# Issue order in a gated DeltaNet scan and of the first two input transfers, in a hybrid encoder layer

## The chip, the cores and the metric

The kernel runs on one core of one Trainium2 chip. The metric is device time in microseconds, the median of several runs. The engines named below are TensorE (PE in the profile, with its weight loads as PEld), VectorE (DVE), ScalarE (ACT), GpSimd (POOL) and SyncE (SP), whose queue issues most of the DMA transfers.

## The reference

One encoder layer over 16 meta tokens and 1024 tokens of width 1024, in float32. A normed input is multiplied with one wide matrix; its columns feed a bidirectional gated DeltaNet with 8 heads (branch A), a short convolution (branch B) and two merge gates. Then come the branch projections, an output projection and a SwiGLU block. The change sits in branch A's scan, which the reference writes as follows, once forwards and once over the reversed sequence:

```python
def step(S, inp):
    qk_c, qd_c, kd_c, u_c, w_c, gl_c = inp
    v_new = u_c - jnp.einsum("bhcd,bhde->bhce", w_c, S)
    o_c = (jnp.einsum("bhcd,bhde->bhce", qd_c, S)
           + jnp.einsum("bhij,bhje->bhie", qk_c, v_new))
    S = S * gl_c[..., None, None] + jnp.einsum("bhcd,bhce->bhde", kd_c, v_new)
    return S, o_c
```

Here u_c and w_c come from a solve with a unit lower triangular matrix, whose inverse the kernel builds beforehand.

## The kernel before

The layer has three stretches. In the first, up to about 923 us, the input projection runs as a stream of dense products (line 328: 128 x 128 weights against 320 to 512 columns, each float32 product split in three), while eight heads pass through norms, inverses and scans beside it. Two further stretches hold the branch projections and the SwiGLU block.

In the first stretch each engine's order of work is the order in which the program issues it, and a small planner decides that order while the program is being built. It keeps a clock for each engine in a table `T`. `pe(ns)` moves TensorE's clock and returns it plus 200; `V(n, kind)` and `A(n)` add an operation's planned time to VectorE's or ScalarE's clock, no earlier than TensorE's, and return that clock plus 370. A stream (the decay, the norms, the inverse or the scan of a head) is a generator. When it yields a time, the main loop goes on with dense products until TensorE's clock has reached it, and only then resumes the stream. `pump()` hands VectorE waiting jobs (convolutions, forward substitutions, norms) while its clock is less than 700 ahead. The planner runs while the kernel is built; on the chip only the order is left, and the semaphores.

A head's scan (`g_scan`, from line 774) takes 8 chunks of 128 tokens in 8 steps; step i works on chunk i forwards and chunk 7 - i backwards. Eight heads make 64 steps. In the first step the backward direction has no state yet, so only the forward one takes part in the products with the state. A step runs so:

- line 853: keys times state, into a PSUM bank b1; line 856: queries times state, into a bank b2
- line 863, VectorE: r0 = values minus the decayed b1, one operation for each direction
- `late`: the product of the step before that is still owed (`inner`, line 892, scores times new values); `outputs()`: its sums into the output on VectorE (line 839) and, once a chunk has been seen from both sides (the outputs of steps 4 to 7, which are issued one step later), their squares on ScalarE (line 843)
- line 871: the inverse (`NP`) times r0, into the other half of b2
- lines 878 and 883, ScalarE: w and v2, two scalings of that result
- line 888: keys times w, into b1; line 902, VectorE: the new state S
- lines 831 and 834: the query part of the output, on ScalarE or VectorE

The scan's PSUM banks come from a ring of three. Each float32 product of the scan shows as two TensorE records, so a group over both directions has four.

At the start of the program nine tiles of 128 rows of x, of 512 KB each, are requested on SP's queue. Tile 0 holds the 16 meta rows and the first 112 rows of x, so two transfers fill it (lines 1049 and 1050). Each tile is squared and summed on ScalarE (line 1073), scaled on VectorE (lines 161 to 168 and 1082) and transposed on TensorE (line 98); the first dense product of line 328 needs three tiles. Before it scales the first tile, VectorE copies the norm's weights out of PSUM (line 1150).

Of the kernel before, what the change touches and what calls it, by code (L numbers as in the profile page):

```python
# [16 lines left out]
P = 128  # L17
# [3 lines left out]
META = 16  # L21
# [27 lines left out]
def encoder_layer(ctx: ExitStack, tc: tile.TileContext, x, meta, norm1_w, w_in, w_ba,  # L49
                  dn_conv_w, A_log, dt_bias, dn_norm_w, sc_conv_w, w_bdn, w_bsc,  # L50
                  w_out, norm2_w, w_gu, w_down, final_w, out):
    nc = tc.nc
    x, out = x[0], out[0]
# [11 lines left out]
    def uid(s):  # L65
        cnt["n"] += 1
        return f"{s}_{cnt['n']}"
# [27 lines left out]
    mm = nc.tensor.matmul  # L95
# [155 lines left out]
    T = {"pe": 0.0, "dve": 0.0, "act": 0.0, "pool": 0.0}  # L251

    def on(e, ns, ready=0.0):

        T[e] = max(T[e], ready, T["pe"]) + ns
        return T[e] + TOPE

    def pe(ns):
        T["pe"] += ns
        return T["pe"] + HOP  # L260

    def V(n, kind=0):
        return on("dve", (68 + 1.042 * n, 130 + 1.042 * n, 130 + 0.52 * n)[kind])

    def A(n):
        return on("act", 144 + 0.834 * n)
# [204 lines left out]
    def cs(c):  # L471
        return slice(META + c * P, META + (c + 1) * P)
# [301 lines left out]
    def g_scan(h, st_):  # L774
        nonlocal freed
        kq, vT, small, kn, NP, PQ, Pm = (st_[k] for k in ("kq", "vT", "small", "kn", "NP", "PQ", "Pm"))
        kT, qT = kq[:, 0], kq[:, 1]
# [6 lines left out]
        def newbank():  # L784
            return pss().rearrange("p (a n) -> p a n", a=4)
# [25 lines left out]
        S = [S0, None]  # L811
# [3 lines left out]
        def outputs():  # L815

            while pending:
                pending.pop(0)()

        def output(b2, c, d, sums):  # L820
            eg = eG[:, c, (h, 8 + h)[d]:(h, 8 + h)[d] + 1]
            first = c not in seen
            seen.add(c)
            if not sums:
                def copy():
                    nc.scalar.copy(oacc[c], b2[:, 2 + d])
                    A(P)
                pending.append(copy)
                return
            if first:  # L830
                nc.scalar.activation(oacc[c], b2[:, d], AF.Copy, scale=eg)
                A(P)
            else:
                nc.vector.scalar_tensor_tensor(out=oacc[c], in0=b2[:, d], scalar=eg, in1=oacc[c],
                                               op0=ALU.mult, op1=ALU.add)
                V(P, 1)

            def add_up():
                nc.vector.tensor_tensor(out=oacc[c], in0=b2[:, 2 + d], in1=oacc[c], op=ALU.add)  # L839
                V(P)  # L840
                if not first:
                    jk = dn.tile([P, P], F32, tag="jk", name=uid("jk"))
                    nc.scalar.activation(jk, oacc[c], AF.Square, accum_out=sso[:, c:c + 1])  # L843
                    on("act", 310)
            pending.append(add_up)

        for i in range(NC):
            cd = (i, NC - 1 - i)
            hd = (h, 8 + h)
            act_ = [d for d in range(2) if S[d] is not None]  # L850
            b1, b2 = newbank(), newbank()
            for d in act_:
                mm(b1[:, d], kT[:, cs(cd[d])], S[d], start=True, stop=True)
            t = pe(215 * len(act_))
            for d in act_:
                mm(b2[:, d], qT[:, cs(cd[d])], S[d], start=True, stop=True)
            pe(215 * len(act_))
            yield t
            r0 = [vS[:, cd[0]], vS[:, cd[1]]]
            for d in act_:  # L860
                c = cd[d]
                r0[d] = dn.tile([P, P], F32, tag=f"r{d}", name=uid("r0"))
                nc.vector.scalar_tensor_tensor(out=r0[d], in0=b1[:, d], scalar=negEG[:, c, hd[d]:hd[d] + 1], in1=vS[:, c],
                                               op0=ALU.mult, op1=ALU.add)
                t = V(P, 1)
            while late:
                late.pop(0)()
            outputs()
            yield t
            for d in range(2):  # L870
                mm(b2[:, 2 + d], NP[:, cd[d], d], r0[d], start=True, stop=True)  # L871
            yield pe(430)
            w = [None, None]
            v2 = [None, None]
            for d in range(2):
                c = cd[d]
                w[d] = dn.tile([P, P], F32, tag=f"w{d}", name=uid("w"))
                nc.scalar.activation(w[d], b2[:, 2 + d], AF.Copy, scale=ce[:, c, d:d + 1])  # L878
                t = A(P)
            for d in range(2):  # L880
                c = cd[d]
                v2[d] = dn.tile([P, P], F32, tag=f"v2{d}", name=uid("v2"))
                nc.scalar.activation(v2[d], b2[:, 2 + d], AF.Copy, scale=cc[:, c, d:d + 1])
                tv = A(P)
            if i < NC - 1:
                yield t
                for d in range(2):
                    mm(b1[:, d], kn[:, cd[d]], w[d], start=True, stop=True)
                t = pe(430)
            def inner(b2=b2, cd=cd, v2=v2):  # L890
                for d in range(2):
                    mm(b2[:, 2 + d], PQ[:, cd[d], d], v2[d], start=True, stop=True)
                return pe(430)
            if i < NC - 1:
                late.append(inner)
                yield t
                for d in range(2):
                    Sn = dn.tile([P, P], F32, tag=f"S{d}", name=uid("S"), bufs=2)
                    if S[d] is None:
                        nc.vector.tensor_copy(Sn, b1[:, d])  # L900
                    else:
                        nc.vector.scalar_tensor_tensor(out=Sn, in0=S[d], scalar=eGl[:, cd[d], hd[d]:hd[d] + 1],
                                                       in1=b1[:, d], op0=ALU.mult, op1=ALU.add)
                    t = V(P, 1)
                    S[d] = Sn
            else:
                yield tv
                t2 = inner()
                freed += 1
                yield t2  # L910

            for d in range(2):
                output(b2, cd[d], d, d in act_)
            yield t
# [50 lines left out]
    def pick():  # L965

        mid = fill_units and fill_units[0][3] in (1, 2)
        if qkv_units and not mid and qkv_ok():
            u = qkv_units.pop(0)
        elif fill_units:  # L970
            u = fill_units.pop(0)
        else:
            return None
        raw = rawtile([P, KT, P])
        nc.sync.dma_start(raw, w_in[unit(u[0])])
        return [u, None, raw, [0]]
# [11 lines left out]
    def start_streams():  # L988
        nonlocal ndec, nnorm, ninv, nscan
        h = ndec  # L990
        if h < H and h < freed + 2 and not decs:
            decs.append([g_decay(h, heads[h]), T["dve"] + HOP, h])
            ndec += 1
        h = nnorm
        if h < H and h < ndec and h < freed + 2 and not norms and all(k in heads[h] and heads[h][k]() for k in ("tk", "tq")):
            norms.append([g_norm(h, heads[h]), T["dve"] + HOP, h])
            nnorm += 1
        h = ninv
        if h < H and not invs and heads[h].get("normed"):
            invs.append([g_inv(h, heads[h]), T["dve"] + HOP, h])  # L1000
            ninv += 1
        h = nscan
        if h < H and not scans and heads[h].get("inverted") and "tv" in heads[h] and heads[h]["tv"]():
            scans.append([g_scan(h, heads[h]), T["dve"] + HOP, h])
            nscan += 1
# [22 lines left out]
    with tc.tile_pool(name="st", bufs=1) as st:  # L1028
# [17 lines left out]
        units = []  # L1046
        for t, xr in enumerate(xs):
            if t == 0:
                nc.sync.dma_start(xr[:META], meta)
                nc.sync.dma_start(xr[META:P], x[0:P - META])  # L1050
            else:
                nc.sync.dma_start(xr[:size(t)], x[P * t - META:P * t - META + size(t)])
            if t == 2:
                units.append(pick())

                nc.sync.dma_start(rows[:120, 0], dn_conv_w[0].rearrange("k (t p) -> (k t) p", p=P))
                nc.sync.dma_start(rows[:24, 1], sc_conv_w[0].rearrange("k (t p) -> (k t) p", p=P))
                nc.sync.dma_start(rows[24:25, 1], dn_norm_w)
                nc.sync.dma_start(raw, w_ba)
            elif t == 5:  # L1060
                units.append(pick())
# [585 lines left out]
    for n, j in enumerate(range(GH + 2, KT - 1), 2):  # L1647
        d = pair_steps(n, j)[0]
# [82 lines left out]
    for t in range(KT - 1):  # L1731
# [3 lines left out]
        xr = m3[2]  # L1735
# [67 lines left out]
    t = KT - 1  # L1803
# [14 lines left out]
    xr = m3[2]  # L1818
# [330 lines left out]
```

## Time and profile before

| | |
|---|---|
| time, median of 3 runs | 1973.54 us (1972.09 to 1974.93) |
| the profiled execution's own time | 1973.36 us |
| its span, first to last instruction | 1971.6 us |
| granted TensorE clock | 1.000 |
| idle time of TensorE before a product, longest single case | 1.5 us, at the start |

The busy shares in the page are averages over the whole span. A busy TensorE row says that products were in flight; how dense they are is read from the distance of their starts in the time-ordered view. There a row joins neighbouring records of one line, with the start of the first, the time to the end of the last, and their number; an idle time ahead of a row stands in brackets with what ended it.

### The profile page before, as it was taken

The numbers are of one execution on the slowest core, as the hardware profiler recorded it, in microseconds if no ns is written. First come the engines' busy times: TensorE is split into PE (matmuls) and PEld (weight loads), VectorE is DVE, ScalarE is ACT, GpSimd is POOL, SyncE is SP. The second block draws the span as 40 slices with busy tenths as digits, with TensorE's granted clock in tenths as the row PEclk, the third lists the DMA queues.
The fourth block names the chain that finished last, engine by engine and source line by source line (L and its number), as shares of the span: only waits on it lengthen the run. The fifth ranks groups of instructions, "written<-read, shape, count | busy, mean of one in ns | idle before, by whom it ended". The sixth has DMA issues, their size and how long they took to land.

```text
span 1971.6 us, 31923 instructions
## 1 busy us (share of the span) xinstructions
PE 1957.3 (99%) x11992; PEld 1719.6 (87%) x11992; DVE 1398.0 (71%) x3017; ACT 837.7 (42%) x1968; POOL 108.4 (5%) x410
## 2 busy tenths in 40 slices
PE   9999999999999999999999999999999999999998
PEld 8999999999999999888888888888888888878887
DVE  7888688888888888845954544468676765746575
ACT  6462364646464646343444211235333333324344
POOL 2011101010101010100000000000000000000000
PEclk9999999999999999999999999999999999999999
DMA  4122121212121212223246642133366654577654
GB/s 145 61 86 81 55 87 60 77 59 77 59 84 52 87 49 87 65 81 108 85 150 242 245 153 86 65 107 112 103 234 246 245 189 153 178 274 242 193 173 168
DMA packets 124704, 251.53 MB, mean 128 GB/s; under 512 B 44988, under 2 KB 46453, under 8 KB 122117
## 3 DMA queue, kind: packets, MB, share of 16 engines
q1 hardware_dynamic: 123957, 248.44, 37.8%
q8 instruction: 94, 1.54, 0.3%
q10 hardware_dynamic: 592, 1.05, 0.1%
q14 instruction: 61, 0.50, 0.1%
HBM read 181.20 MB, written 68.25 MB: 127 GB/s over the span
## 4 chain that ended last, share of the span: by engine, by line
PE 45%; DMA 3%; DVE 2%; ACT 1%; issue 0%; SPq 0%; DVEq 0%; ACTq 0%
PE pd L1446 12%; PE pe L1446 6%; PE pm L1446 4%; PE pe L2057 1%; PE pe L2055 1%; PE pe L2056 1%; PE pd L2057 1%; PE pd L2055 1%; PE pd L2056 1%; PE pe L134 1%; PE pe L135 1%; PE pd L135 1%; PE pd L134 1%; PE pe L136 1%; PE pd L136 1%; PE pm L2056 1%
## 5 line engine op out<-in xcount | busy, mean ns | idle before, releaser
L328 PE MATMUL pm<-hTh,wh 128*128 128x320 f32 (+4 forms) x1248 | 426.9, 347 | 0.3 <-ACT hTh L1096 0.2
L328 PE MATMUL pm<-hTh,wl 128*128 128x320 f32 (+4 forms) x1248 | 426.8, 347 | 0.0
L328 PE MATMUL pm<-al,wh 128*128 128x320 f32 (+4 forms) x1248 | 423.8, 345 | 0.0
L328 PEld LDWEIGHTS pm<-hTh,wh 128*128 128x128 f32 x1248 | 233.9, 188 | 10.7 <-ACT hTh L1096 0.9
L328 PEld LDWEIGHTS pm<-al,wh 128*128 128x128 f32 x1248 | 233.8, 188 | 10.7
L328 PEld LDWEIGHTS pm<-hTh,wl 128*128 128x128 f32 x1248 | 233.9, 188 | 10.2 <-POOL wl L1111 0.3
L102 DVE TENSOR_TENSOR al<-raw,ring_h 128x1024 fp32r<-128x1024 f32 x73 | 88.6, 1222 | 65.6 <-ACT ring_h L101 64.7
L101 ACT CAST ring_h<-raw 128x1024 fp32r<-128x1024 f32 x73 | 76.6, 1053 | 109.1 <-PE pe L2057 35.0
L982 DVE TENSOR_TENSOR wl<-raw,wh 128x512 fp32r<-128x512 f32 x112 | 75.3, 687 | 34.5 <-ACT wh L985 34.2
L350 DVE SCALAR_TENSOR_TENSOR kq<-ra,wc,kq 128x520 f32<-128x520 f32 x128 | 96.5, 754 | 3.5 <-ACT kq L380 2.0
L878 ACT ACTIVATE w<-pd,small 128x128 f32<-128x128 f32 x128 | 39.8, 362 | 123.4 <-PE pd L871 122.9
L483 DVE TENSOR_TENSOR tm<-fP,fN 128x135 f32<-128x135 f32 (+23 forms) x248 | 72.2, 291 | 4.8
L487 DVE TENSOR_TENSOR fP<-fP,tm 128x135 f32<-128x135 f32 (+23 forms) x248 | 71.9, 290 | 5.0
L985 ACT CAST wh<-raw 128x512 fp32r<-128x512 f32 x112 | 66.3, 624 | 3.8 <-issue 3.6
L101 ACT CAST wh<-raw 128x1024 fp32r<-128x1024 f32 x37 | 38.8, 1047 | 47.8 <-PE pe L135 10.4
L1994 ACT ACTIVATE b<-b 128x512 f32<-128x512 f32 x20 | 12.6, 632 | 101.6 <-DVE b L1412 101.6
L843 ACT ACTIVATE jk<-NP 128x128 f32<-128x128 f32 x64 | 19.9, 311 | 81.1 <-DVE NP L839 80.1
L102 DVE TENSOR_TENSOR wl<-raw,wh 128x1024 fp32r<-128x1024 f32 x37 | 45.1, 1219 | 10.2 <-ACT wh L101 10.0
L1446 PE MATMUL pd<-b_hl,wh 128*128 128x512 f32 x168 | 51.9, 390 | 0.0
L1412 DVE TENSOR_TENSOR b<-pd,b 128x512 f32<-128x512 f32 x21 | 14.5, 689 | 52.5 <-PE pd L1446 47.5
L350 DVE SCALAR_TENSOR_TENSOR vT<-ra,wc,vT 128x520 f32<-128x520 f32 x64 | 48.3, 754 | 1.4 <-ACT vT L380 0.7
L679 POOL TENSOR_TENSOR tm<-mP,mN 1x15 f32<-1x15 f32 (+7 forms) x120 | 36.9, 307 | 210.8 <-DMA mN<-ndm 202.4
(630 smaller groups left out, 4772.1 us busy)
## 6 DMA issues: line engine op xcount, KB each, us to landing
raw<-in_w_in_dram SPq DMA_DIRECT2D x72, 512.0 KB
raw<-in_w_gate_up_dram SPq DMA_DIRECT2D x44, 512.0 KB
sums<-in_w_down_dram SPq DMA_DIRECT2D x22, 512.0 KB
t_d<-sums SPq DMA_DIRECT2D x11, 1024.0 KB
raw<-s_d SPq DMA_DIRECT2D x44, 256.0 KB
raw<-t_d SPq DMA_DIRECT2D x44, 256.0 KB
act_d<-b SPq DMA_DIRECT2D x43, 256.0 KB
raw<-act_d SPq DMA_DIRECT2D x33, 256.0 KB
```

Source lines behind the costliest of these rows:

```text
L101: nc.scalar.copy(hi, src)
L102: nc.vector.tensor_tensor(out=lo, in0=src, in1=hi.bitcast(F32), op=ALU.subtract)
L134: mm(po[:m, :n], wh[:, k, :m], xhk[:, t0:t0 + n], start=(k == 0), stop=False)
L328: mm(po[:, :n], ww[:, k], f(k)[:, t0:t0 + n], start=i == 0, stop=i == 3 * KT - 1)
L350: nc.vector.scalar_tensor_tensor(out=acc, in0=raw[:, h0 + t:h0 + t + hn], scalar=wc[:, t, col:col + 1], in1=acc, op0=ALU.mult, op1=ALU.add)
L483: nc.vector.tensor_tensor(out=tv, in0=fP[:, 0:r, j:j + 1].broadcast_to([P, r, n]), in1=fN[:, j:j + 1, j + 1:32].broadcast_to([P, r, n]), o ...
L487: nc.vector.tensor_tensor(out=fP[:, 0:r, j + 1:32], in0=fP[:, 0:r, j + 1:32], in1=tv, op=ALU.subtract)
L878: nc.scalar.activation(w[d], b2[:, 2 + d], AF.Copy, scale=ce[:, c, d:d + 1])
L982: nc.vector.tensor_tensor(out=u[1][1][:, k], in0=u[2][:, k], in1=u[1][0][:, k].bitcast(F32), op=ALU.subtract)
L985: nc.scalar.copy(u[1][0][:, k], u[2][:, k])
L1446: mm(po, x[:, k], at(y, k), start=i == 0 and not add_to, stop=i == 11, skip_group_check=add_to)
L2056: mm(bank[t], h_[:, c], l_[:, hi], start=False, stop=False)
```

## The change

Two places are edited. In the scan step the products of line 856 are issued behind the r0 operations of line 863 instead of ahead of them, and the pause between the two is gone. The pause ahead of line 871 is kept only where the planned end of r0 (with its margin) lies more than 150 ns behind TensorE's planned clock; otherwise line 871's products follow at once. At the start, the transfer of the 112 rows of x is requested ahead of the 16 meta rows.

```diff
@@ -851,11 +851,7 @@
             b1, b2 = newbank(), newbank()
             for d in act_:
                 mm(b1[:, d], kT[:, cs(cd[d])], S[d], start=True, stop=True)
-            t = pe(215 * len(act_))
-            for d in act_:
-                mm(b2[:, d], qT[:, cs(cd[d])], S[d], start=True, stop=True)
             pe(215 * len(act_))
-            yield t
             r0 = [vS[:, cd[0]], vS[:, cd[1]]]
             for d in act_:
                 c = cd[d]
@@ -863,10 +859,14 @@
                 nc.vector.scalar_tensor_tensor(out=r0[d], in0=b1[:, d], scalar=negEG[:, c, hd[d]:hd[d] + 1], in1=vS[:, c],
                                                op0=ALU.mult, op1=ALU.add)
                 t = V(P, 1)
+            for d in act_:
+                mm(b2[:, d], qT[:, cs(cd[d])], S[d], start=True, stop=True)
+            pe(215 * len(act_))
             while late:
                 late.pop(0)()
             outputs()
-            yield t
+            if t > T["pe"] + 150:
+                yield t
             for d in range(2):
                 mm(b2[:, 2 + d], NP[:, cd[d], d], r0[d], start=True, stop=True)
             yield pe(430)
@@ -1046,8 +1046,8 @@
         units = []
         for t, xr in enumerate(xs):
             if t == 0:
+                nc.sync.dma_start(xr[META:P], x[0:P - META])
                 nc.sync.dma_start(xr[:META], meta)
-                nc.sync.dma_start(xr[META:P], x[0:P - META])
             else:
                 nc.sync.dma_start(xr[:size(t)], x[P * t - META:P * t - META + size(t)])
             if t == 2:
```

## The prediction

> **What bounds the kernel now.** I read the page first, then the list of TensorE's waits, then busy times by stretch, then the time-ordered view of single steps of the scan.
>
> ```profile
> span 1971.6 us, 31923 instructions
> PE 1957.3 (99%) x11992; PEld 1719.6 (87%) x11992; DVE 1398.0 (71%) x3017; ACT 837.7 (42%) x1968; POOL 108.4 (5%) x410
> ...
> PE pe L590 <- DVE PQ L629: 1.1, 2, 0.8
> ...
> 400.00:600.00 200.00, 200.00 (x1711) 191.74 (x1710) 173.06 (x515) 106.03 (x351) 23.18 (x94) 1.00 0.23 68
> ...
> 850.00:900.00 50.00, 49.85 (x477) 41.68 (x476) 19.94 (x51) 21.68 (x60) 0.00 (x0) 1.00 0.26 80
> ```
>
> The wait rows give the waiting line, who released it, total us, times and the longest; the last two rows are stretches with span, then busy time of PE, PEld, DVE, ACT, POOL, granted clock, DMA share and GB/s. The reader is to see that TensorE is the resource: 200.00 of 200 us busy in the middle of the scans, at full clock, and only 1.1 us of waiting on the scans' stage. TensorE runs its list in order, so a microsecond counts only if a product is removed, made cheaper, or waits less.
>
> Now one scan step (a head's sixth, i = 5), both directions. Columns: start, duration, engine, line, operation, count.
>
> ```profile
> 899.57 0.39 PE L328 MATMUL pm<-al,wh 128*128 128x512 f32 x1
> 899.80 0.61 PE L853 MATMUL pd<-S,kq 128*128 128x128 f32 x4
> 900.24 0.61 PE L856 MATMUL pd<-S,kq 128*128 128x128 f32 x4
> 900.69 0.61 PE L892 MATMUL pd<-v,PQ 128*128 128x128 f32 x4
> 901.05 0.48 PE L328 MATMUL pm<-hTh,wl 128*128 128x512 f32 x1
> 901.37 0.39 PE L328 MATMUL pm<-hTh,wh 128*128 128x512 f32 x1
> 901.60 0.39 PE L328 MATMUL pm<-al,wh 128*128 128x512 f32 x1
> 901.83 0.60 PE L871 MATMUL pd<-r,NP 128*128 128x128 f32 x4
> 902.20 0.48 PE L328 MATMUL pm<-hTh,wl 128*128 128x512 f32 x1
> 902.51 0.40 PE L328 MATMUL pm<-hTh,wh 128*128 128x512 f32 x1
> ...
> 903.42 0.61 PE L888 MATMUL pd<-w,kn 128*128 128x128 f32 x4
> ...
> 900.44 0.61 DVE L863 SCALAR_TENSOR_TENSOR r<-pd,negEG,vS 128x128 f32<-128x128 f32 x2 [0.48 <-PE pd L853]
> 901.34 0.49 DVE L839 TENSOR_TENSOR NP<-pd,NP 128x128 f32<-128x128 f32 x2 [0.28 <-PE pd L892]
> ...
> 901.66 0.31 ACT L843 ACTIVATE jk<-NP 128x128 f32<-128x128 f32 x1 [1.53 <-DVE NP L839]
> ...
> 902.48 0.63 ACT L878 ACTIVATE w<-pd,small 128x128 f32<-128x128 f32 x2
> ...
> L863 DVE SCALAR_TENSOR_TENSOR r<-pd,negEG,vS x120: 338/343/353, 216.9 to 912.6; 128x128 f32<-128x128 f32 x120
> ```
>
> The scan's groups (four records each) stand between dense products (L328) that cover its latency. The last row gives L863's count, its least, median and greatest ns, and the first and last start. No row of PE carries an idle time: the three dense products ahead of L871 are useful work, not waiting.
>
> **The change, part by part.** *Scan.* L856 moves behind the r0 operations, and when the planner thinks VectorE prompt, the inverse's products (L871) follow L892 without the three or four dense products between. The planner's own figures: with b1 issued at T0, TensorE's clock is T0 + 430, the two r0 operations add 2 x 263 and the margin is 370, so t = T0 + 1326; after L856 and a late inner product TensorE's clock is T0 + 1290. The excess of 36 is under 150, so a VectorE planned at most 114 late gives no pause; a later one gives the old pause from the same t. Before, r0 was planned from T0 + 860, so t was T0 + 1756 and 466 ns of dense products came between: the three above. A head's first step has one direction and no inner product: t exceeds TensorE's clock by 418, the pause stays, 215 shorter.
>
> Removed from TensorE: nothing. Does joining make the group cheaper? From 899.57 to 901.37 stand two dense products (0.23 each, 901.37 to 901.60) and three groups: 1.80 - 0.46 = 1.34, or 0.447 a group. From 901.60 to 902.51 stand two dense products and L871 alone: 0.91 - 0.46 = 0.45. A group costs the same alone or joined, so the saving is 0 (by the rounding of these rows at most 0.01 in each of 8 x 7 two-direction steps, 0.6 us). The cover is the dense work itself, which is only put elsewhere; gone, it would cost what L871 waits for r0.
>
> Does L871 then wait for r0? It would start at 899.80 + 3 x 0.447 = 901.14; the r0 pair ends at 900.44 + 0.61 = 901.05. No. The first direction's products need only the first r0, 0.34 long in the last row, ready at 900.78, 0.36 ahead; the second's have 0.22 more than the pair's end shows. The planner lets VectorE be 0.11 late at most, so I price this at 0; where VectorE is later on the chip than planned, up to 0.3 us a step.
>
> What is late next? L871 comes 0.69 earlier, L888 too (903.42 becomes 902.73), for the planner keeps the dense products between them. But w (L878) is ScalarE's, and from i = 5 on ScalarE has the squares of the previous step's outputs (L843) in front of it. Those hang on L839, which hangs on L892, and L892 doesn't move. So w still starts at 902.48. How soon after w can L888 run?
>
> ```profile
> L878 ACT ACTIVATE w<-pd,small x128: 347/360/377, 218.3 to 915.3; 128x128 f32<-128x128 f32 x128
> ...
> 834.70 0.58 ACT L447 ACTIVATE rb<-pm 128x512 f32<-128x512 f32 x1
> ...
> 835.18 0.61 ACT L878 ACTIVATE w<-pd,small 128x128 f32<-128x128 f32 x2
> ...
> 835.59 0.56 PEld L888 LDWEIGHTS pd<-w,kn 128*128 128x128 f32 x4 [0.19 <-ACT w L878]
> 835.67 0.66 PE L888 MATMUL pd<-w,kn 128*128 128x128 f32 x4
> ...
> 541.14 0.61 PE L853 MATMUL pd<-S,kq 128*128 128x128 f32 x4
> ...
> 543.06 0.60 PE L871 MATMUL pd<-r,NP 128*128 128x128 f32 x4
> ...
> 543.81 0.61 ACT L878 ACTIVATE w<-pd,small 128x128 f32<-128x128 f32 x2
> ...
> 544.82 0.60 PE L888 MATMUL pd<-w,kn 128*128 128x128 f32 x4
> ...
>   PE pd L853: 12.0, 18
> ```
>
> At 835 the weight load waits for the first w, which ends at 835.18 + 0.36 = 835.54; the product starts at 835.67, 0.13 later. So in the step above L888 can't start before 902.48 + 0.36 + 0.13 = 902.97: **TensorE stands still 0.24 us**, and everything behind it in its list, the dense products too, waits; the state update and the next step come later by as much. In the 320- and 384-column stretches the shift is smaller: at 541 L871 would be at 541.14 + 1.34 = 542.48, 0.58 earlier, L888 at 544.24, against 543.81 + 0.49 = 544.30: 0.06. If an eviction stands between squares and w, as L447 does at 834.70, the product that now just fits waits for the whole shift, 0.69. So a stall costs 0.06 to 0.69; I take 0.24, the plain case.
>
> How many? The last row above says that in 18 of the 64 steps VectorE stood idle for L853; those surely join. Three steps of each eight (i = 5, 6, 7) have the squares: 24 of 64. 18 x 24/64 = 7 steps; with the 114 ns of tolerance some not quite idle ones follow, so I take 9, between 7 and 24. 9 x 0.24 = **+2.2 us**.
>
> [...]
>
> *Opening.* The two transfers of the first tile swap places on SP's queue.
>
> ```profile
> 0.81 0.41 SPq L1049 DMA_DIRECT2D xr<-in_meta_tokens_dram  x1
> 1.27 0.40 SPq L1050 DMA_DIRECT2D xr<-in_x_dram  x1
> ...
> 5.29 1.06 ACT L1073 ACTIVATE jk<-xr 128x1024 f32<-128x1024 f32 x1 [2.35 <-DMA xr<-in_x_dram]
> ...
> 6.04 0.69 DVE L1150 COPY w1row<-pm 128x512 f32<-128x512 f32 x1 [0.16 <-PE pm L98]
> ...
> 6.86 0.17 DVE L161 RECIPROCAL ss<-ss 128x1 f32<-128x1 f32 x1
> ...
> 13.51 0.89 PE L328 MATMUL pm<-hTh,wh 128*128 128x336 f32 x4
> ```
>
> The large one is asked for 0.46 earlier and the small one 0.46 later; the later tiles' keep their place. ScalarE's first square waits for the tile, so it may start up to 0.46 earlier; but VectorE is in the copy L1150 until 6.73 and takes L161 at 6.86, so at most 0.13 comes through. If the small transfer, now second, ends the tile, the loss is at most its 0.46. I take -0.1, the gain nearest the rows, since what ended the wait was the large transfer.
>
> **The sum**: 0 (work) + 2.2 (stalls) - 0.1 (opening) = +2.1 us. It is made against the profiled execution's own time, 1973.36 us (span 1971.6 and 1.8 around it), which lies 0.18 under the median of the runs, 1973.54. That gives **1975.5 us**, 0.1% over. About 0.2%, 3.9 us, is what a measurement here can tell from no change.
>
> **Rivals.** *The pause stays* (the change doesn't do what it says): VectorE, 173 of 200 us busy in the middle, is mostly planned too late, so few steps join. For it: only 18 idle cases. Against: those 18, most steps with no other vector work at the end. Time: 1973.36 - 0.1 = 1973.3.
>
> *ScalarE's queue becomes the bound* (slower): w sits behind squares and an eviction or a cast in many joined steps, each at up to 0.69; 12 such steps cost 8.3 us, 1981.5. For it: the row at 834.70 and L888's weight load, already waiting there. Against: at 541 the price is 0.06. It decides from 6 steps at 0.69, or 17 at 0.24, which is 4 us.
>
> *The scan's length sets the phase's end* (faster): the last head's steps are 0.69 shorter; seven of them, 4.8 us, less 0.1 of the opening is 1968.5.
>
> ```profile
> 922.82 0.40 PE L328 MATMUL pm<-hTh,wl 128*128 128x512 f32 x1
> 923.05 1.04 PE L98 MATMUL pd<-ident,NP 128*128 128x128 f32 x8
> 923.85 0.48 PE L136 MATMUL pe<-hTh,wl 128*128 128x512 f32 x1
> ```
>
> For it: the fill work ends just where the last head's outputs are transposed (L98). Against: dense products run up to that point and the next phase's (L136) follow at once, so an earlier scan leaves the same products to do. [...]
>
> **How the numbers follow.** Forecast (9 or so short stalls) 0.47; the pause stays 0.18; ScalarE's queue 0.25; the scan's end 0.10. Of the forecast 0.04 lies over +3.9 us, of the last case 0.01 under 3.9 us of gain. Faster 0.09; same 0.43 + 0.18 + 0.01 = 0.62; slower 0.25 + 0.04 = 0.29. Range: the low end is no stall, the 1.1 us at L590 gone and 0.13 of the opening, 1972.1, drawn to 1971.3 to take in part of the fast case; the high end is 10 stalls at 0.69, 6.9 us, 1980.3, put at 1980.
>
> **What would show it.** Right: in joined steps L871 directly behind L892 without idle time, three or four dense products fewer between; new waits of L888 (or of the last step's L892) for ScalarE of some 0.06 to 0.69 each, 1 to 4 us together; a square or two in front of each such w; the start of the first L328 0.1 earlier than 13.51. Wrong: L871 waiting for VectorE, which would mean that the room for r0 is less than 0.3; a group's cost under 0.44 when joined; the last transposes earlier together with everything behind them, which would mean that the scan's end counted.

## The result and the profile after

The changed kernel takes 1981.29 us (median of 6 runs, 1979.93 to 1983.46) against 1974.94 us for the kernel before on the same chip (6 runs, 1972.09 to 1976.74): a ratio of 1.0034, 95% interval 1.0022 to 1.0047. It is slower, by some 6.3 us or 0.3%. The forecast was 1975.5 us, at most 1980, with a chance of 0.62 on no change beyond some 3.9 us and 0.29 on slower.

The page of the changed kernel, and busy times by stretch (span, then PE, PEld, DVE, ACT, POOL, clock, DMA share, GB/s):

```profile
span 1981.7 us, 31927 instructions
PE 1963.1 (99%) x11992; PEld 1719.4 (87%) x11992; DVE 1401.3 (71%) x3017; ACT 836.0 (42%) x1968; POOL 107.0 (5%) x410
```

```profile
400.00:600.00 200.00, 198.59 (x1689) 188.39 (x1688) 171.89 (x506) 102.86 (x343) 23.00 (x94) 1.00 0.21 67
600.00:800.00 200.00, 199.27 (x1697) 189.69 (x1696) 172.04 (x504) 103.83 (x344) 23.49 (x94) 1.00 0.23 70
```

The number of products is the same (11992), and so is the clock (1.00 in these stretches of both kernels). But between 400 and 600 us, where TensorE was busy for 200.00 of 200 us, it now stands 1.41. Against the kernel before (span 1971.6) the 10.1 us of span divide so: the first dense product starts 0.87 later (14.38 against 13.51), the stage from the first to the last dense product of line 328 is 8.13 longer (917.44 against 909.31), and what follows is 1.12 longer (1049.91 against 1048.79). The profiled execution of the changed kernel is the slowest of its six (1983.46 us), so its 10.1 is more than the 6.3 of the medians. The 8 us of the stage are no chance of that execution: scan_only below, profiled at its median, has a stage of 917.34.

Whom does TensorE wait for? First the waits of PE between 200 and 940 us in the changed kernel, then who waited for the new state (line 902), with us and times; the last two rows are the kernel before's.

```profile
PE pd L853 <- DVE S L902: 1.7, 3, 0.6
PE pd L98 <- DVE NP L928: 0.5, 1, 0.5
PE pd L892 <- ACT v L883: 0.2, 1, 0.2
```

```profile
L902 DVE SCALAR_TENSOR_TENSOR S<-S,eGl,pd x104: 331/340/349, 220.6 to 915.1; 128x128 f32<-128x128 f32 x104
...
  PEld pd L853: 4.7, 12
  PE pd L853: 1.7, 3
```

```profile
L902 DVE SCALAR_TENSOR_TENSOR S<-S,eGl,pd x104: 330/340/348, 220.0 to 911.0; 128x128 f32<-128x128 f32 x104
...
  PEld pd L853: 0.5, 1
```

The reader is to see a wait that the prediction did not list: the next step's first group (L853) stands for S. The list of PE's waits shows only the part in which PE had nothing in flight; its weight loads wait 4.7 us in 12 places, against 0.5 in one.

To size all such stalls alike, I took for every product of the scan's groups the distance of its start from the start of the product ahead, less the usual one (0.231 us behind a dense product of 512 columns, 0.1745 of 384, 0.1545 of 336, 0.147 of 320, 0.111 behind another scan product), and summed what exceeds 25 ns. By this measure the change adds 4.39 us at L853 (0.49 to 4.88), 1.15 at L892 (0.41 to 1.56), 0.88 at L871 (0 to 0.88) and 0.60 at L888 (0.04 to 0.64): 7.0 of the 8.1 us.

One step shows how S gets late. Here are TensorE, ScalarE and VectorE of the changed kernel:

```profile
542.07 0.60 PE L871 MATMUL pd<-r,NP 128*128 128x128 f32 x4
...
545.39 0.61 PE L888 MATMUL pd<-w,kn 128*128 128x128 f32 x4
...
549.07 0.75 PE L853 MATMUL pd<-S,kq 128*128 128x128 f32 x4 [0.64 <-DVE S L902]
```

```profile
542.21 0.31 ACT L843 ACTIVATE jk<-NP 128x128 f32<-128x128 f32 x1 [1.78 <-DVE NP L839]
...
543.29 0.64 ACT L355 ACTIVATE rb<-kq 128x520 f32<-128x520 f32 x1 [0.24 <-DVE kq L350]
543.83 0.60 ACT L985 CAST wh<-raw 128x512 fp32r<-128x512 f32 x1
544.34 0.62 ACT L878 ACTIVATE w<-pd,small 128x128 f32<-128x128 f32 x2
544.85 0.62 ACT L883 ACTIVATE v<-pd,small 128x128 f32<-128x128 f32 x2
545.35 0.63 ACT L985 CAST wh<-raw 128x512 fp32r<-128x512 f32 x1
```

```profile
544.47 0.69 DVE L982 TENSOR_TENSOR wl<-raw,wh 128x512 fp32r<-128x512 f32 x1 [0.31 <-ACT wh L985]
545.08 0.30 DVE L487 TENSOR_TENSOR fP<-fP,tm 128x144 f32<-128x144 f32 x1
546.01 0.69 DVE L982 TENSOR_TENSOR wl<-raw,wh 128x512 fp32r<-128x512 f32 x1 [0.63 <-ACT wh L985]
...
548.67 0.60 DVE L902 SCALAR_TENSOR_TENSOR S<-S,eGl,pd 128x128 f32<-128x128 f32 x2
```

Line 985 is ScalarE's cast of the next weights to their high part, line 982 VectorE's subtraction that makes the low part; they are issued at four fixed places in the dense products of one unit of the projection (`SPL = (33, 36, 39, 42)`: cast, subtraction, cast, subtraction). In this step the first cast stands behind two squares and a tanh (L355), the second behind w and v. VectorE has the subtractions in its queue and stands 0.31 and 0.63 us for the casts, 0.94 in all, more than the stall that follows. The product behind S (L888) ended by 546.00, long before; S comes at 548.67 because VectorE's queue is late, and L853 stands 0.64.

The same step (the fourth head, i = 6) in the kernel before, where its L853 starts at 541.14:

```profile
540.12 1.12 ACT L985 CAST wh<-raw 128x512 fp32r<-128x512 f32 x2
```

```profile
540.02 0.60 DVE L902 SCALAR_TENSOR_TENSOR S<-S,eGl,pd 128x128 f32<-128x128 f32 x2
540.54 0.60 DVE L834 SCALAR_TENSOR_TENSOR NP<-pd,eG,NP 128x128 f32<-128x128 f32 x2
541.06 0.68 DVE L982 TENSOR_TENSOR wl<-raw,wh 128x512 fp32r<-128x512 f32 x1
```

There both casts ran one behind the other ahead of VectorE, the subtraction found its cast done and stood behind S, and L853 started 0.52 after the pair of S operations had ended (540.62), without a wait.

Not every stall of L853 is of this kind. One step earlier VectorE stands for an eviction (L380, ScalarE's scaled copy of a finished product out of PSUM); S is late behind that, and L853 starts at 539.85 with 0.26 us of excess:

```profile
537.90 0.76 DVE L350 SCALAR_TENSOR_TENSOR kq<-ra,wc,kq 128x520 f32<-128x520 f32 x1 [0.50 <-ACT kq L380]
...
539.45 0.60 DVE L902 SCALAR_TENSOR_TENSOR S<-S,eGl,pd 128x128 f32<-128x128 f32 x2
```

Of the 4.88 us at L853 in the changed kernel, 2.86 stand in four steps in which VectorE waited for a cast between r0 and S (0.94, 0.94, 0.63 and 0.95 us, for excesses of 0.78, 0.94, 0.25 and 0.89). 1.26 stand in six steps in which it waited 0.44 to 0.64 for L380, 0.39 in two with an eviction of its own that waited for a dense product (L438), and 0.37 in three steps without such a wait. Of the kernel before's 0.49 all stands behind casts. So the casts explain some 2.4 of the 4.39 added, and evictions most of the rest.

What the prediction did describe is there too. A joined step late in the scans:

```profile
907.09 0.61 PE L892 MATMUL pd<-v,PQ 128*128 128x128 f32 x4
907.54 0.61 PE L871 MATMUL pd<-r,NP 128*128 128x128 f32 x4
907.90 0.48 PE L328 MATMUL pm<-hTh,wl 128*128 128x512 f32 x1
...
908.50 0.31 ACT L843 ACTIVATE jk<-NP 128x128 f32<-128x128 f32 x1
...
908.81 0.61 ACT L878 ACTIVATE w<-pd,small 128x128 f32<-128x128 f32 x2
908.92 0.39 PE L328 MATMUL pm<-hTh,wh 128*128 128x512 f32 x1
909.21 0.75 PE L888 MATMUL pd<-w,kn 128*128 128x128 f32 x4
```

L871 follows L892 by 0.45, w stands behind the squares, and L888 starts 0.29 behind its dense product in place of 0.23. 17 of the 64 steps are joined.

### The profile page after: what moved, and what is told of

Its sections match the earlier page's. It is cut to its first block, busy times and chain, and to the rows that moved or that the text cites. A ratio compares the mean times of both kernels' runs of the same rounds, so it can differ in the third digit from the quotient of the medians.

```text
span 1981.7 us, 31927 instructions
## 1 busy us (share of the span) xinstructions
PE 1963.1 (99%) x11992; PEld 1719.4 (87%) x11992; DVE 1401.3 (71%) x3017; ACT 836.0 (42%) x1968; POOL 107.0 (5%) x410
## 4 chain that ended last, share of the span: by engine, by line
PE 52%; DMA 3%; DVE 3%; issue 1%; ACT 1%; SPq 0%; DVEq 0%; ACTq 0%
PE pd L1446 11%; PE pe L1446 5%; PE pm L1446 4%; PE pm L328 4%; PE pe L135 2%; PE pe L134 2%; PE pe L136 2%; PE pe L2056 1%; PE pe L2057 1%; PE pe L2055 1%; PE pd L2056 1%; PE pd L2057 1%; PE pd L2055 1%; PE pd L135 1%; PE pd L134 1%; DMA sums<-in_w_down_dram 1%
## 5 line engine op out<-in xcount | busy, mean ns | idle before, releaser
L328 PEld LDWEIGHTS pm<-al,wh 128*128 128x128 f32 x1248 | 233.9, 188 | 10.5
L982 DVE TENSOR_TENSOR wl<-raw,wh 128x512 fp32r<-128x512 f32 x112 | 75.8, 686 | 31.3 <-ACT wh L985 30.8
L985 ACT CAST wh<-raw 128x512 fp32r<-128x512 f32 x112 | 67.1, 628 | 3.7 <-issue 3.6
L101 ACT CAST wh<-raw 128x1024 fp32r<-128x1024 f32 x37 | 38.8, 1048 | 47.4 <-PE pe L135 10.5
L859 DVE SCALAR_TENSOR_TENSOR r<-pd,negEG,vS 128x128 f32<-128x128 f32 x120 | 36.7, 344 | 15.4 <-PE pd L853 15.1
```

What stands on the lines that cost most here:

```text
L101: nc.scalar.copy(hi, src)
L328: mm(po[:, :n], ww[:, k], f(k)[:, t0:t0 + n], start=i == 0, stop=i == 3 * KT - 1)
L982: nc.vector.tensor_tensor(out=u[1][1][:, k], in0=u[2][:, k], in1=u[1][0][:, k].bitcast(F32), op=ALU.subtract)
L985: nc.scalar.copy(u[1][0][:, k], u[2][:, k])
```

## Experiments

All kernels are measured against the kernel before on their chip, whose median lies between 1972.7 and 1974.9 us, so ratios are to be compared rather than times. "Stage" is the time from the first to the last start of line 328's products, the other columns are the excess sums of the section above, all in us and from one profiled execution each. "Scan edit" is the first hunk of the change alone, with the old order of the two transfers.

```
                              time    ratio (95% interval)       stage   L853  L888  L892  L871
kernel before                                                    909.3   0.49  0.04  0.41  0
the change                    1981.29 1.0034 (1.0022 to 1.0047)  917.4   4.88  0.64  1.56  0.88
dma_only                      1974.13 1.0003 (0.9994 to 1.0012)  909.2   0.33  0.06  0.41  0
scan_only                     1981.36 1.0037 (1.0025 to 1.005)   917.3   4.65  0.64  1.58  0.85
scan_pause                    1974.83 1.0007 (0.9998 to 1.0016)  911.9   2.69  0.33  0.17  1.92
scan_clock                    1977.01 1.0012 (1.0003 to 1.0021)  912.2   1.21  0.97  0.59  0.43
clock_squares                 1977.85 1.0018 (1.0009 to 1.0027)  916.1   5.32  0     0     1.84
nudge_pause                   1977.32 1.0015 (1.0006 to 1.0024)  913.1   1.61  0.31  0.42  0
nudge_split (30,33,36,39)     1979.41 1.0029 (1.0019 to 1.004)   917.7   4.23  0.18  0.06  0.04
scan_split30 (same)           1978.24 1.0023 (1.0014 to 1.0033)  916.0   4.68  0.80  0.60  0.35
before_split36 (36,39,42,45)  1982.18 1.0042 (1.0028 to 1.0055)  917.2   3.58  0.06  0.25  0.47
scan_split36 (same)           1983.12 1.0044 (1.0027 to 1.0062)  919.6   4.27  0.50  0.98  1.03
before_gap (30,36,39,45)      1975.82 1.0010 (1.0 to 1.0019)     913.3   0.96  0     0.56  0.04
scan_gap (same)               1971.98 0.9987 (0.9978 to 0.9997)  910.2   0.62  0.75  0.64  0.90
after_gap (same)              1971.58 0.9989 (0.998 to 0.9998)   909.9   0.52  0.75  0.63  0.91
```

**Which half of the change?** dma_only swaps the two transfers in the kernel before; scan_only is the rest.

```diff
+                nc.sync.dma_start(xr[META:P], x[0:P - META])
                 nc.sync.dma_start(xr[:META], meta)
-                nc.sync.dma_start(xr[META:P], x[0:P - META])
```

> The kernel before with the two first transfers swapped and nothing else. In the changed kernel the first dense product started at 14.38 us instead of 13.51. If the swap makes the first tile land later, the first dense product starts 0.5 to 1 us later here too and the time rises by as much, 0.03 to 0.05%. If that was chance of one execution, it starts at 13.5 give or take 0.2 and the time stays within 0.3 us.

> The scan's edit without the swap. All theories of the scan expect the larger part of the loss, +5 to +6 us (+0.25 to 0.3%), with the last dense product of the first stretch some 7 us later than before. If the swap were the cause, within 1 us of before.

dma_only stays within what can be told from no change, and scan_only loses what the whole change loses: the loss is the scan edit's. A second single run of dma_only (dma_again) took 1972.72 us.

> The swap of the two first transfers alone, once more, to see how the opening varies between executions. If the swap makes the first tile land later, the first dense product starts at 14.2 us or later, against 13.4 to 13.6 in the kernels of this call with the old order. If it is chance, both orders show starts of 13.4 to 14.4 us mixed; one execution with the old order has shown 14.31 already.

In the opening, ScalarE's rows of the changed kernel, then of dma_again:

```profile
5.61 1.06 ACT L1073 ACTIVATE jk<-xr 128x1024 f32<-128x1024 f32 x1 [2.66 <-DMA xr<-in_meta_tokens_dram]
...
8.12 1.06 ACT L1073 ACTIVATE jk<-xr 128x1024 f32<-128x1024 f32 x1 [0.97 <-DMA xr<-in_x_dram]
```

```profile
5.58 1.06 ACT L1073 ACTIVATE jk<-xr 128x1024 f32<-128x1024 f32 x1 [2.65 <-DMA xr<-in_meta_tokens_dram]
...
7.03 1.04 ACT L1073 ACTIVATE jk<-xr 128x1024 f32<-128x1024 f32 x1
```

The 16 meta rows, now second, end the first tile (the wait names their transfer), and the first square starts at 5.61 and 5.58; in dma_only and after_gap, with the new order too, it starts at 5.15 and 5.20, with the old order at 5.29 (before) and 5.17 (scan_only). So it is neither clearly earlier nor later. The second tile's rows were late in one execution and not in the other. The first dense product starts at 14.38 (the change), 14.23 (dma_only), 13.80 (dma_again) and 13.41 (after_gap) with the new order, at 13.38 to 14.85 in the executions with the old one: the order makes no difference that stands out from this scatter.

**Joining, or the earlier booking of r0?** scan_pause always pauses ahead of L871, so no step joins; scan_clock joins as the change does but sets the planner's clock of VectorE to what the old booking would have given.

```diff
 scan_pause
-            if t > T["pe"] + 150:
-                yield t
+            yield t
 scan_clock
             pe(215 * len(act_))
+            v0 = T["dve"]
             r0 = [vS[:, cd[0]], vS[:, cd[1]]]
...
             pe(215 * len(act_))
+            T["dve"] = max(v0, T["pe"]) + 263.4 * len(act_)
             while late:
```

> The scan's edit with the pause ahead of the inverse's products kept in every step, so that no step joins; r0 is still planned 430 ns earlier on the planner's VectorE clock than before. Theory A (the planner's VectorE clock now runs ahead of the chip, VectorE is overbooked, and the products with the state wait for it): the loss stays, +4 to +6 us, with waits of line 853 of 3 to 5 us in sum. Theory B (joined steps run into ScalarE's squares): the loss goes, within 1 us of before. Theory C (any other order of this stretch loses, for the order of before happens to fit): somewhere between 0 and +6 us, with waits at places of their own.

> The scan's edit with the same rule for joining, but the planner's VectorE clock is set, behind r0, to what the kernel before booked for it (r0 from the clock behind both products with the state). Theory A: the waits of line 853 fall back under 1 us and the time to within +1.5 us of before, with steps still joined. Theory B: the joined steps still wait for w, +3 to +6 us. Theory C: between 0 and +6 us.

Both come out between, 1974.83 and 1977.01, and neither falls where theory A put it. It looked as if each half of the edit had a price of its own. But scan_pause has more excess at L853 than scan_clock (2.69 against 1.21) although its median is lower. Nor do the times separate the two: their stages are 911.9 and 912.2, and the profiled executions, the fastest of the one (1972.67 us) and the slowest of the other (1978.39), differ in what follows the stage (1044.7 and 1050.9 us), where no line was changed.

**Control: shift the old order.** nudge_pause lengthens the pause ahead of L871 in the kernel before by 100 of the planner's ns; nudge_split moves the four parts of the weight split three dense products earlier. Neither joins a step or books r0 earlier. clock_squares is scan_clock with the squares issued behind w and v, so that w stands behind none.

```diff
 nudge_pause
-            yield t
+            yield t + 100
 nudge_split
-    SPL = (33, 36, 39, 42)
+    SPL = (30, 33, 36, 39)
 clock_squares: line 843's operation, with its line on("act", 310), leaves outputs() as
-                    nc.scalar.activation(jk, oacc[c], AF.Square, accum_out=sso[:, c:c + 1])
+                    squares.append(c)
 and is issued for every c in squares behind
                 tv = A(P)
```

> The kernel before with the pause ahead of the inverse's products lengthened by 100 ns on the planner's clock: no joining, no earlier booking, only another order of the stretch. Theory A (early booking on the planner's VectorE clock costs): waits at the heads of the scan's groups stay near the 0.9 us of before and the time within 1 us. Theory C (any other order loses, since the order of before happens to fit): waits of 2 to 5 us and +1 to +4 us.

> The kernel before with the four places at which the next unit's weights are split moved three products earlier: another order, with the scan's planning untouched. Theory A: waits at the heads of the scan's groups under 2 us, time within 1 us. Theory C: waits of 2 to 5 us, +1 to +4 us.

> The scan's edit with VectorE booked as before, and the squares issued behind w and v2 instead of ahead of them. If what is left of the loss (3.2 us of waits, 0.97 of them of line 888 for w) is w behind the squares, the waits for w fall under 0.2 us and the time to +1 to +2.5 us over before. If the squares don't matter, the waits for w stay near 1 us and the time near +2.4 to +3.8 us. If joining itself gains once both are mended, at or under the time of before.

The kernel before loses 3.2 and 5.3 us from shifts without joining or earlier booking, nudge_split with 4.23 us at L853. And with L888's wait for w gone altogether clock_squares has 5.32 at L853 and is no faster than scan_clock. That is above the +1 to +2.5 us expected, if w behind the squares were what is left. So the stalls that the prediction priced are not the main loss, and joining and booking need not be; with the old booking the excess at L853 can be as large as with the new. What is common is L853 behind S.

**Misses: mending VectorE's wait in other ways.** In the aware kernels the planner books the subtraction no earlier than its cast ends; in the pool kernels GpSimd subtracts, and the split stands at 24, 27, 30, 33. Each was made of the scan edit and of the kernel before.

```diff
 scan_aware, before_aware
             nc.scalar.copy(u[1][0][:, k], u[2][:, k])
             A(512)
+            u[3][1:] = [T["act"]]
...
+            T["dve"] = max(T["dve"], u[3][1] + HOP)
             V(512)
 scan_pool, before_pool
-            nc.vector.tensor_tensor(out=u[1][1][:, k], in0=u[2][:, k], in1=u[1][0][:, k].bitcast(F32), op=ALU.subtract)
-            V(512)
+            nc.gpsimd.tensor_tensor(out=u[1][1][:, k], in0=u[2][:, k], in1=u[1][0][:, k].bitcast(F32), op=ALU.subtract)
-    SPL = (33, 36, 39, 42)
+    SPL = (24, 27, 30, 33)
```

> The scan's edit, and the planner now books VectorE's subtraction of the next unit's weights (line 982) no earlier than the end of ScalarE's cast (line 985) that it needs; the operations stay the same. Theory D (VectorE stands in its queue waiting for ScalarE's casts, which the planner doesn't know, so the new state and with it line 853 come later than planned): waits of line 853 fall from 4.6 to under 2 us, time to +2 to +5 us over before. Theory A (early booking of r0): waits of line 853 stay at 3 to 5 us, time at +6 to +8. Theory C (order by chance): anything from +1 to +8.

> The kernel before with the same booking of the subtraction. Theory D: waits of line 853 under 1.5 us although the order of the stretch is new, time within 1.5 us of before. Theory C: as in the two nudges, waits of 2 to 5 us and +2 to +5 us.

> The scan's edit with the subtraction of the next unit's weights moved from VectorE to GpSimd, and the four places of the split nine products earlier for GpSimd's slower operation (1.29 us instead of 0.69). VectorE then has nothing in its queue that waits for the casts, and 75 us less work. Theory D: waits of line 853 under 1 us, time at or up to 2 us over before; if joined steps gain anything, under before. Theory B (joined steps behind the squares): waits for w and v stay or grow, 1 to 3 us. New risk: dense products that wait for GpSimd's low half of the weights.

> The kernel before with the same move to GpSimd. Theory D: waits of line 853 under 0.5 us, time from 1 us under to 1 us over before. Theory C: +1 to +4 us. Against scan_pool it shows what the scan's edit alone is worth once VectorE no longer waits for the casts: by theory D within 1 us, by theories A and B 3 to 6 us more with the edit.

All four are much slower: 2033.84 us (ratio 1.0301, 1.0287 to 1.0315), 1997.80 (1.0119, 1.0105 to 1.0132), 2013.18 (1.0194, 1.018 to 1.0208) and 2003.93 (1.0146, 1.0133 to 1.016). scan_aware has 1.79 us at L853 in place of 4.65 as long as there are dense products, but these end at 902.8 while the scans run on to 987, and without dense work their latency is bare; the granted clock falls there too. Its row between 940 and 980 us (29.56 of 40 us busy, at a clock of 0.75), and its longest wait of PE:

```profile
940.00:980.00 40.00, 29.56 (x205) 25.53 (x205) 13.69 (x46) 14.13 (x50) 0.00 (x0) 0.75 0.00 1
```

```profile
PE pm L134 <- ACT wh L1499: 10.1, 1, 10.1
```

The likely reason is that a clock that charges these waits to VectorE, with nothing else re-timed, makes the plan late; this wasn't traced. The pool kernels speak against theory D as it was put: no subtraction is left in VectorE's queue, yet L853 has 6.1 us (scan_pool) and 7.8 (before_pool), where under 1 and 0.5 were expected. VectorE's own operations last longer in before_pool (line 350: at most 0.82 us in the kernel before, up to 1.875 there; last section), and the split stands elsewhere, so the four runs decide nothing between the theories.

**The place of the split, in both orders.** The same shifts were laid on the scan edit, and a shift the other way on both.

```diff
-    SPL = (33, 36, 39, 42)
+    SPL = (30, 33, 36, 39)   scan_split30
+    SPL = (36, 39, 42, 45)   before_split36, scan_split36
+    SPL = (30, 36, 39, 45)   before_gap, scan_gap, after_gap
```

> The scan edit alone (old order of the two transfers) with the split three products earlier. If the edit has a cost of its own (early booking, joining): the loss adds to that of the shift, 1979.4 + 7 = 1986 us, or at least 1981. If the place decides: the new order is off by some products from the old, and this place may fit it better or worse; 1975 to 1983, not the sum.

> The kernel before with the weight split three products later (36, 39, 42, 45 in place of 33, 36, 39, 42). If the place of the split against the scan step decides: the old place is no optimum by design, so this loses as the earlier shift did, 1976 to 1981 us, with 2 to 5 us of waits of L853 for S. If the loss belongs to the scan edit: 1974 us, and under 1.5 us of waits.

> The scan edit alone with the split three products later. Edit's own cost: 3 us or more over the kernel before with the same split, 1981 us or more if that one stands at 1978. Place: at one of the two shifted places the scan edit comes within 3 us of the kernel before, 1974 to 1977, with L853's waits for S under 2.5 us (4.65 at the old place).

At 30 the scan edit and the old order are equal (1.0023 and 1.0029), at 36 too (1.0044 and 1.0042). The edit's 0.37% is there only where the split stands at 33, the place of the kernel before. No loss was added to another: the sum of shift and edit, 1986 us, did not come. But the other half of the expectation failed too: no shifted place brought the scan edit to 1974 to 1977. A shift keeps cast and subtraction three products apart, and all of these have 3.6 to 4.7 us at L853, of which 2.2 to 3.1 stand in steps in which VectorE waited for a cast between r0 and S.

**Cast and subtraction further apart.** The last set leaves six products between each cast and its subtraction: the first cast comes three products earlier, the second subtraction three later.

> The kernel before with the split at 30, 36, 39, 45: six products instead of three between a cast and its subtraction. If VectorE's wait for the cast makes S late: nothing to win here, as the old order has 0.5 us of such waits of L853; 1973 to 1976 us. If only the place counts, whatever VectorE waits for: 1976 to 1980, as with the other shifts.

> The scan edit alone with six products between a cast and its subtraction. If VectorE's wait for the cast is the cause: L982's idle time on VectorE falls, L853's waits for S go from 4.65 to under 2 us, and the time from 1981.4 to 1975 to 1978 us. If it is not (early booking or joining, or the evictions): 1980 us or more, with 4 us or more of waits of L853.

> The whole change (scan edit and new order of the two transfers) with the split at 30, 36, 39, 45. If the loss came from VectorE's waits for the casts: as scan_gap, 1971 to 1974 us, L853's waits under 1.5 us (4.88 in the changed kernel), first dense product up to 0.9 later. If scan_gap was one lucky place: 1976 us or more.

Who VectorE's subtraction waited for, and who waited for S, in scan_only and then in scan_gap:

```profile
L982 DVE TENSOR_TENSOR wl<-raw,wh x112: 671/687/736, 43.9 to 915.3; 128x512 fp32r<-128x512 f32 x112
...
  ACT wh L985: 30.7, 29
```

```profile
  PEld pd L853: 4.6, 11
  PE pd L853: 1.7, 3
```

```profile
L982 DVE TENSOR_TENSOR wl<-raw,wh x112: 670/685/750, 44.3 to 899.6; 128x512 fp32r<-128x512 f32 x112
...
  ACT wh L985: 17.2, 19
```

```profile
  PEld pd L853: 0.6, 2
```

The scan edit goes from 1981.36 to 1971.98 us, further than expected, and L853's waits go with it; the whole change with this split (after_gap) takes 1971.58, 0.9989 of the kernel before (0.998 to 0.9998). These two are the fastest kernels of the study, 2.2 and 2.5 us under the kernel before. Both still book r0 early and join 15 steps, so neither costs the 7 us by itself. In none of the stalls of L853 that are left in the three gap kernels did VectorE wait for a cast between r0 and S. But in scan_gap the stalls behind L380, 1.28 us in scan_only, are gone as well, though nothing about evictions was edited; so this set doesn't separate the casts' share from that of another order. The total of L982's waits is no measure by itself: the kernel before has 34.2 us of them in 25 places, with room behind them:

```profile
L982 DVE TENSOR_TENSOR wl<-raw,wh x112: 671/684/778, 44.1 to 908.6; 128x512 fp32r<-128x512 f32 x112
...
  ACT wh L985: 34.2, 25
```

What counts is whether S stands in VectorE's queue behind one, as in the step at 546.01 above (VectorE stood 0.63 us, then L853 0.64).

## Why the prediction was wrong

*No product is saved by joining: right.* In the joined step above L892 to L871 is 0.45, as a group alone; over the 17 joints the first product of L871 comes 0.11 behind the last of L892, as inside a group.

*L871 doesn't wait for r0: right where steps join, incomplete elsewhere.* Over all joints the excess is 0.01 us. The 0.88 at L871 stands in other steps, mainly at 521.55 (0.28 us) and 818.70 (0.45), where the shorter pause now ends before VectorE is there. The prediction priced only joined steps.

*The 18 idle steps "surely join": 17 joints, but not these.* Two of the 18 rows with VectorE idle for L853 belong to first steps of a head, which the prediction's own rule leaves apart, and four others didn't join; five steps that it hadn't counted did. The number is near by luck.

*w behind the squares, 9 stalls of 0.24, +2.2 us: the mechanism is there, the sum near by luck.* L888 added 0.60 us and L892 of a head's last step, which follows v at once, 1.15: together 1.75. In all ten steps with such a stall ScalarE had two squares ahead of w and v. But the joints aren't spread evenly over a head's steps, as the 24/64 supposed: 14 of the 17 are in steps without squares, eight of them at i = 1. Three joined steps with squares stall, by 0.20, 0.26 and 0.32 us, so the price of one was about right and the number, nine, was not. The other seven stalls, 1.42 us, are in steps that did not join, where the pause is only shorter; the prediction had no term for them. clock_squares takes both shares away and gains nothing, so they were not what decided.

*The opening, -0.1: not shown.* The small transfer, second, ends the tile, which the prediction had as its other bound; the effect is lost in the scatter of the start.

*What failed* is the step "What is late next?". It followed L871 to L888 and ended at "the state update and the next step come later by as much": a new state later by the shift only, with ScalarE's and VectorE's other work where it was. But the edit books r0 earlier and shortens the step, so the planner hands both engines their jobs at other places of the step, and the weight split, tied to the count of dense products, meets another part of it. The planner books the subtraction without waiting for the cast; so nothing in the plan shows that VectorE will stand, and S, behind it, reaches L853 late. L853 behind a late S was 4.39 of the 7.0 us, some 2.4 of it behind casts and most of the rest behind evictions, and the range had no term for it: its upper end counted stalls of L888 alone. The row that should have opened the term was in the profile of before: VectorE waited 34.2 us for L985 in 25 places without harm to L853 but for 0.5 us, so one had to ask what a shift would do to that.

*The rivals.* "ScalarE's queue becomes the bound" gave 1981.5 us, near the result by luck: it counted 12 stalls of L888 at 0.69, and L888 has 0.64 in all, L892 1.56. ScalarE's queue does decide for the larger part, but through VectorE's waits for casts and evictions. "The pause stays" falls with the 17 joints, "the scan's end" with dense products that run to the end of the stage as before.

*How far this is shown.* That the loss is not the edit's own price is shown by four places of the split, at which edit against old order gives about +8, -1, +1 and -4 us (the differences of the medians). That VectorE's wait for the cast makes S late is shown in the rows of the step, and scan_gap takes both away together. But moving parts of the split moves other work too; the stalls behind evictions come and go with it, and before_gap, with only 0.96 us at L853, is still 4 us longer in its stage than the kernel before. Some 2.1 us of that are two waits of TensorE inside the inverse (lines 741 and 738, 1.3 and 0.8 us) that the kernel before doesn't have; why they arise stays open. That the gap is a better place in general is therefore not shown. Nor is it shown that the gap kernels beat the kernel before in this stage: the stages of scan_gap and after_gap are 0.9 and 0.5 us longer than before's, and their gain comes from what follows, 1046.5 and 1046.3 us against 1048.8, where no line was changed and where the profiled executions of the table range from 1044.7 to 1050.9.

## What to carry to other kernels

Where the order of every engine is fixed when the program is built, an edit of a few instructions is also a shift of everything placed by a clock or a count; before crediting or blaming the edit, shift the old kernel by as much with an edit that should do nothing. Where one engine's operation hangs on another engine's, try more room between the two when they are issued (it took 9 us off the scan edit here and added 2 to the kernel before), for a wait in VectorE's queue was paid by whatever stood behind it (0.94 us of waits, then 0.64 at L853, in the step shown). A wait that costs nothing today may have slack only at its present place: 34.2 us of VectorE's waits for casts went with 0.49 us at L853 in the kernel before, 30.7 us with 4.65 in scan_only.

## What the hardware showed unasked

In before_pool a subtraction takes 1.29 us on GpSimd in the median (0.684 on VectorE), and some of VectorE's operations beside it take longer. Both engines of before_pool at one place, then the convolution's operations of line 350 (least, median, greatest ns) of before and before_pool:

```profile
494.20 3.31 POOL L982 TENSOR_TENSOR wl<-raw,wh 128x512 fp32r<-128x512 f32 x2 [4.15 <-ACT wh L984]
...
494.72 4.14 DVE L350 SCALAR_TENSOR_TENSOR vT<-ra,wc,vT 128x520 f32<-128x520 f32 x3
```

```profile
L350 DVE SCALAR_TENSOR_TENSOR kq<-ra,wc,kq x128: 742/753/820, 45.3 to 753.8; 128x520 f32<-128x520 f32 x128
```

```profile
L350 DVE SCALAR_TENSOR_TENSOR kq<-ra,wc,kq x128: 742/754/1875, 40.5 to 782.7; 128x520 f32<-128x520 f32 x128
```

Three operations that take 0.75 each take 4.14 while GpSimd makes two subtractions. Of the 192 operations of this line, 20 last over 1 us, and each of these lies beside a subtraction on GpSimd; the longest of those that touch none takes 0.83. But 23 others overlap a subtraction by up to 0.53 us in the trace and keep their 0.75, so how much of a subtraction lengthens them, and by what means, is not shown. Work moved to GpSimd was not free for VectorE: the 192 operations took 164.0 us in all, 144.8 in the kernel before. The scan's groups of before_pool have 10.5 us of excess against 0.94, but the split was moved too, so the share of the long operations in that is open.
